# A decoder layer on one core: rotary on 128 partitions with rows moved by DMA, decays by one addition, squares on ScalarE, longer waits in the delta rule

## The chip, the cores and the metric

The kernel runs on one core of a Trainium2 chip. The metric is the device time of one execution in microseconds. Five engines work side by side, each on its own queue in order: TensorE (PE, with its weight loads PEld), VectorE (DVE), ScalarE (ACT), GpSimd (POOL) and SyncE (SP). SP, ACT and POOL also issue DMA transfers; here SP loads the weights and POOL moves small tiles about.

## The reference, cut to what matters

One layer of a hybrid decoder, 256 tokens of width 2048, all in float32:

```python
h = rms_norm(x, ln1)
proj = h @ w_in                     # GDN q|k|v, beta, decay, gate z, MoBA q|k|v, two branch gates
y_a = gated_deltanet(...) @ w_branch_a       # 8 heads of 128, chunks of 64
y_b = moba_attention(partial_rope(q), partial_rope(k), v) @ w_branch_b
x = x + (sigmoid(gate_a) * y_a + sigmoid(gate_b) * y_b) @ w_out
x = x + gated_mlp(rms_norm(x, ln2))          # width 5632, causal conv of 3
out = rms_norm(x, final_norm)
```

Two pieces of it are touched by the change. Partial rotary turns the first 32 of each head's 128 dimensions, with x1 the first 16 and x2 the next 16, and an angle of position times frequency:

```python
rot = concatenate([x1 * cos - x2 * sin, x2 * cos + x1 * sin])
```

The delta rule works on differences of summed decays: `gamma = exp(where(causal, gc[c] - gc[s], -inf))`, then a triangular solve per chunk, a running state, and a normalisation of each head's output by the mean of its squares.

## The kernel before, in words

Activations lie with channels on the 128 partitions and the 256 tokens along the free dimension. Every float32 product is made of three faster ones: a weight block of 128x2048 comes in by SP (L123), ACT rounds it to a high part wh (L113), DVE subtracts to get the low part wl (L110, two instructions of 128x1024 per block), and PE adds high x high, high x low and low x high (L103, 48 matmuls per output block of 128 channels). High and low parts have two buffers each, the raw weight four.

The layer runs in this order: the first projections and the norm; four groups of two delta-rule heads (q, k, v and z, `gdn` and `z` in the names); four groups of two MoBA heads (`moba` for q and k, `v` for v); 16 blocks of gates; the two branch products (`br`); the output product (`wo`); the MLP (`up`, `pd`). Beside this stream of large matmuls stand generators: `decay` (L371), one `gdn` per group (L439), `rotary` (L320) and one `moba` per group (L658). A generator writes a few instructions and yields. The function `tick` (L95) advances every living generator by one step, and it is called each time the main stream has written matmuls worth 1700 units, that is every 16 matmuls of 256 columns. `yield from wait(n)` lets n such steps pass.

The order so written isn't the order on the engines. `TileContext(nc, schedule_with_timeline_sim=True)` has a planner that walks through the program with its own idea of each instruction's time, and gives each engine the instruction written earliest among those it believes ready. On the chip that order is fixed, and an instruction that turns out not to be ready holds up all that stands behind it on its engine. A tile with a `tag` shares its buffers with the other tiles of that tag; a new one waits until an old one is released.

What the change and the prediction's steps touch:

- `rotary` loads the positions into `posi` (48 partitions x 256, in the buffer of tag `ot`, L321-322), makes angles on partitions 0 to 15 and 32 to 47, reduces them by multiples of 2 pi in some thirty DVE steps (`turns`, `less`), and takes sine and cosine on ACT (L365-368).
- `moba` turns q and k (L659-663): two DVE products of 16x512 into `rt`, a POOL product of 48x512 with the cosine and a POOL addition. The columns of the q and k weights are permuted on the host so that x1 and x2 stand at partitions 0 and 32. Three waits later come the scores (L669).
- `gdn` brings two rows of the summed decays to all partitions (`gam`, L441), squares q on POOL (`sqq`, L443), sums the squares on PE (`ssq`), makes three blocks of decay differences per head with six DVE instructions (L454-458, with the columns `cols` and the causal mask `nm`) and one exponential (L459).
- The triangular solve goes through DRAM several times: `X` to `dX` to `Xr` (L528, L530), then `rows` (L534-536) uses `Xr` at L547, four waits after L546; `dE`, `E` and `UB` follow (L550-556), and the chain of products L584 to L604 (`w0`, `z0`, `w1`).
- At the end of a group `ot` is squared on POOL and summed on DVE (L614-615), scaled (L616-619), and after four waits (L620) transposed on PE (`pot`, L624).

Of the kernel before, what the change touches and what calls it, by code (L numbers as in the profile page):

```python
# [11 lines left out]
F32 = mybir.dt.float32  # L12
F32R = mybir.dt.float32r
I32 = mybir.dt.int32
# [5 lines left out]
P = 128  # L20
# [19 lines left out]
def const_array():  # L40
# [3 lines left out]
    c["nm"] = np.where(i[None, :] >= i[:, None], 0.0, -30000.0)  # L44
# [9 lines left out]
    invf = np.zeros((P, 1))  # L54
    invf[:16, 0] = inv
    invf[32:48, 0] = -inv
    c["invf"] = invf
# [18 lines left out]
def layer_kernel(ctx: ExitStack, tc: tile.TileContext, xT, pos, cst, vec, convw, ffw, bdv,  # L76
# [226 lines left out]
    sint = fk.tile([48, T], F32, name="sint")  # L303
    cost = fk.tile([48, T], F32, name="cost")
    rem = cost[:16, :P]
# [5 lines left out]
    rt = fk.tile([48, 2, T], F32, name="rt")  # L311
    pool.memset(rt, 0.0)
# [7 lines left out]
    def rotary():  # L320
        posi = g.tile([48, T], I32, name="posi", tag="ot", bufs=1)  # L321
        sp.dma_start(posi, pos)
        ang = m.tile([48, T], F32, name="ang", tag="s_")
        dve.tensor_copy(ang, posi)
        dve.tensor_scalar(ang, ang, C["invf"][:48, :], None, op0=ALU.mult)
        qn = m.tile([48, T], F32, name="qn", tag="s_")
# [9 lines left out]
        lo1 = m.tile([48, T], F32, name="lo1", tag="pT_")  # L336
        lo2 = m.tile([48, T], F32, name="lo2", tag="pT_")
# [27 lines left out]
        act.activation(sint, ang, AF.Sin)  # L365
        act.activation(cost, ang, AF.Sin, scale=0.5)
        dve.tensor_tensor(cost, cost, cost, op=ALU.mult)
        dve.tensor_scalar(cost, cost, -2.0, 1.0, op0=ALU.mult, op1=ALU.add)


    def decay():  # L371
# [27 lines left out]
        pool.dma_start(dG, gc)  # L399
        dve.tensor_scalar(rem, gc[:, :P], gc[:, P - 1:P], -1.0, op0=ALU.subtract, op1=ALU.mult)  # L400
# [8 lines left out]
        dve.tensor_copy(cols.rearrange("p a b -> p (a b)"), pt[:, :112])  # L409

# [14 lines left out]
    dG = dr.tile([16, T], F32, name="dG", bufs=1)  # L425
    S1 = fk.tile([P, 2, P], F32, name="S1")
# [5 lines left out]
    def dram(t, offset, *ap):  # L432
        return bass.AP(tensor=t.tensor, offset=t.offset + offset, ap=[list(x) for x in ap])

    def wait(n):
        for _ in range(n):
            yield

    def gdn(h0, kq, v):  # L439
# [3 lines left out]
        pool.tensor_tensor(sq, kq[:, 1], kq[:, 1], op=ALU.mult)  # L443
# [7 lines left out]

        for j in range(2):
            c = 8 + h0 + j
            dve.scalar_tensor_tensor(gam[:, j, 2, :], gam[:, j, 1, :], cols[:, 1, c:c + 1], nm,  # L454
                                     op0=ALU.subtract, op1=ALU.min)
            dve.tensor_scalar(gam[:, j, 1, :], gam[:, j, 1, :], cols[:, 2, c:c + 1], 0.0, op0=ALU.add, op1=ALU.min)
            dve.scalar_tensor_tensor(gam[:, j, 0, :], gam[:, j, 0, :], cols[:, 0, c:c + 1], nm,
                                     op0=ALU.subtract, op1=ALU.min)
        act.activation(gam, gam, AF.Exp)  # L459
# [86 lines left out]
        yield from wait(4)  # L546
# [67 lines left out]
        pool.tensor_tensor(so, ot, ot, op=ALU.mult)  # L614
        dve.tensor_reduce(st[:, 4, :], so, axis=AX.X, op=ALU.add)
# [4 lines left out]
        yield from wait(4)  # L620
# [37 lines left out]
    def moba(h0, q, k, v):  # L658
        for t in (q, k):  # L659
            dve.tensor_tensor(rt[:16], t[32:48], sint[32:48, None, :].to_broadcast([16, 2, T]), op=ALU.mult)  # L660
            dve.tensor_tensor(rt[32:48], t[:16], sint[:16, None, :].to_broadcast([16, 2, T]), op=ALU.mult)
            pool.tensor_tensor(t[:48], t[:48], cost[:, None, :].to_broadcast([48, 2, T]), op=ALU.mult)
            pool.tensor_tensor(t[:48], t[:48], rt, op=ALU.add)
# [219 lines left out]
def blocks(w, cw=P):  # L883
    k, n = w.shape
    return w.reshape(k // P, P, n // cw, cw).transpose(2, 1, 0, 3).reshape(n // cw, P, k // P * cw)
# [59 lines left out]
```

## Time and profile before

| | |
|---|---|
| median of 3 runs | 1471.27 us (1469.22 to 1472.8) |
| the profiled execution, its own time | 1470.49 us |
| its span, first to last instruction | 1468.7 us, mean granted TensorE clock 0.996 |
| busy PE, PEld | 1445.5 us (98%), 1387.4 us (94%) |
| busy DVE, ACT, POOL | 971.6 us (66%), 727.1 us (50%), 171.9 us (12%) |
| DMA | 280.52 MB, mean 191 GB/s |

The busy shares are means over stages that differ: the delta rule and MoBA lie between about 40 and 410 us, and the rest is the stream of large matmuls alone. Matmuls are pipelined, so a busy PE is PE with a matmul in flight. The number in brackets behind a row of a timeline is the engine's idle time just before it and what ended it. A plain float32 matmul shows as two instructions.

### The profile page before, as it was taken

To read this page: it belongs to the slowest core of one execution; us is meant where nothing else is said; L and a number is where in the kernel's file an instruction comes from. 1 tells how busy PE (TensorE), PEld (TensorE's weight loads), DVE (VectorE), ACT (ScalarE), POOL (GpSimd) and SP (SyncE) were. 2 spreads that over 40 slices of the span, in tenths; PEclk is the share of its full clock that TensorE was granted. 3 is DMA by queue.
4 is the path that set the end of the run, shared out by engine and by line. 5 is a ranking of instruction groups with operands and counts; after the bars stand their busy time and mean duration, and the time that the engine had idled before them with its cause. 6 is when DMAs were issued, how large, how long until landed. Compare 5 with 4: busy or idle time off the path is not lost.

```text
span 1468.7 us, 26659 instructions
## 1 busy us (share of the span) xinstructions
PE 1445.5 (98%) x11264; PEld 1387.4 (94%) x11264; DVE 971.6 (66%) x1395; ACT 727.1 (50%) x994; POOL 171.9 (12%) x208
## 2 busy tenths in 40 slices
PE   9999999999999999999999999999999999999997
PEld 8999999888999999999999999999999998888886
DVE  7989889886754555766666666666666665554554
ACT  5665673445554444445455544454455454444444
POOL 0023134341230000100100000000000000000000
PEclk9999999999999999999999999999999999999999
DMA  9466554554455555567555555555555555555552
GB/s 338 161 196 200 194 180 154 172 170 156 156 189 191 187 197 201 180 221 262 201 181 193 201 196 186 193 201 193 187 196 201 193 186 173 195 201 195 184 194 86
DMA packets 45319, 280.52 MB, mean 191 GB/s; under 512 B 6544, under 2 KB 7824, under 8 KB 13072
## 3 DMA queue, kind: packets, MB, share of 16 engines
q1 hardware_dynamic: 40272, 270.40, 53.4%
q0 software_dynamic: 4064, 6.26, 1.6%
q10 hardware_dynamic: 864, 2.16, 0.4%
q8 instruction: 88, 1.44, 0.4%
q14 instruction: 31, 0.25, 0.1%
HBM read 275.30 MB, written 3.75 MB: 190 GB/s over the span
## 4 chain that ended last, share of the span: by engine, by line
PE 86%; DVE 6%; DMA 3%; ACT 2%; issue 2%; POOL 1%; SPq 0%; DVEq 0%; POOLq 0%; ACTq 0%
PE ps_up L103 33%; PE pd L91 16%; PE ps_gate L103 12%; PE ps_wo L103 6%; PE ps_br L103 6%; PE ps_gdn L103 4%; PE ps_moba L103 3%; PE ps_v L103 2%; DVE wl L110 2%; PE ps_z L103 2%; DMA wraw<-in_w_gdn 1%; DMA Xr<-dX 1%; ACT wh L113 1%; DMA dX<-X 1%; DVE tm L521 1%
## 5 line engine op out<-in xcount | busy, mean ns | idle before, releaser
L110 DVE TENSOR_TENSOR wl<-wraw,wh 128x1024 fp32r<-128x1024 f32 (+1 forms) x500 | 607.0, 1250 | 183.1 <-ACT wh L113 182.5
L113 ACT CAST wh<-wraw 128x1024 fp32r<-128x1024 f32 (+1 forms) x500 | 496.0, 1040 | 411.2 <-PE ps_up L103 161.0
L103 PE MATMUL ps_up<-h,wh 128*128 128x256 f32 x2816 | 479.4, 276 | 0.0
L103 PEld LDWEIGHTS ps_up<-h,wh 128*128 128x128 f32 x2816 | 424.0, 188 | 0.1
L103 PE MATMUL ps_up<-h,wl 128*128 128x256 f32 x1408 | 388.7, 276 | 0.0
L103 PEld LDWEIGHTS ps_up<-h,wl 128*128 128x128 f32 x1408 | 264.3, 188 | 0.0
L103 PE MATMUL ps_gate<-hc,wh 128*128 128x256 f32 x1024 | 175.5, 277 | 0.0
L103 PEld LDWEIGHTS ps_gate<-hc,wh 128*128 128x128 f32 x1024 | 154.5, 188 | 0.0
L103 PE MATMUL ps_gate<-hc,wl 128*128 128x256 f32 x512 | 141.6, 277 | 0.0
L91 PE MATMUL pd<-wl,ah 128*128 128x512 f32 x336 | 130.8, 389 | 0.0
L91 PE MATMUL pd<-wh,al 128*128 128x512 f32 x336 | 130.8, 389 | 0.0
L103 PE MATMUL ps_gdn<-hc,wh 128*128 128x256 f32 x704 | 125.0, 280 | 0.0
L103 PEld LDWEIGHTS ps_gdn<-hc,wh 128*128 128x128 f32 x704 | 107.6, 189 | 0.4 <-ACT wh L113 0.4
L103 PE MATMUL ps_gdn<-hc,wl 128*128 128x256 f32 x352 | 98.4, 280 | 1.8 <-DVE wl L110 1.8
L103 PEld LDWEIGHTS ps_gate<-hc,wl 128*128 128x128 f32 x512 | 96.1, 188 | 0.1
L103 PE MATMUL ps_moba<-hc,wh 128*128 128x256 f32 x512 | 93.3, 284 | 0.0
L91 PE MATMUL pd<-wh,ah 128*128 128x512 f32 x336 | 92.8, 391 | 0.0
L203 DVE TENSOR_TENSOR unf<-ps_up,R 128x512 f32<-128x512 f32 x44 | 30.4, 692 | 89.0 <-PE ps_up L103 89.0
L103 PE MATMUL ps_wo<-mc,wh 128*128 128x256 f32 x512 | 87.1, 276 | 0.0
L816 POOL TENSOR_TENSOR acts<-sg,cvf 128x256 f32<-128x256 f32 x44 | 32.4, 737 | 459.4 <-ACT sg L815 459.4
L103 PEld LDWEIGHTS ps_moba<-hc,wh 128*128 128x128 f32 x512 | 79.6, 191 | 0.2
L103 PEld LDWEIGHTS ps_wo<-mc,wh 128*128 128x128 f32 x512 | 77.0, 188 | 0.0
(437 smaller groups left out, 1995.7 us busy)
## 6 DMA issues: line engine op xcount, KB each, us to landing
wraw<-in_w_up SPq DMA_DIRECT2D x88, 1024.0 KB, 4.9
wraw<-in_w_dn SPq DMA_DIRECT2D x44, 1024.0 KB, 4.8
wraw<-in_w_gate SPq DMA_DIRECT2D x32, 1024.0 KB, 4.8
wraw<-in_w_gdn SPq DMA_DIRECT2D x30, 1024.0 KB, 5.2
wraw<-in_w_moba SPq DMA_DIRECT2D x16, 1024.0 KB, 4.9
wraw<-in_w_o SPq DMA_DIRECT2D x16, 1024.0 KB, 4.9
wraw<-in_w_mv SPq DMA_DIRECT2D x8, 1024.0 KB, 5.1
wraw<-in_w_ba SPq DMA_DIRECT2D x8, 1024.0 KB, 4.9
```

Source lines behind the costliest of these rows:

```text
L91: pe.matmul(ps, a, b, start=(start and i == 0), stop=(stop and i == n - 1), **kw)
L103: pe.matmul(ps, a, b, start=start, stop=stop, skip_group_check=True)
L110: return (eng or dve).tensor_tensor(lo, src, hi.bitcast(F32), op=ALU.subtract)
L113: act.copy(hi, src)
L203: dve.tensor_tensor(dst, ps, r, op=ALU.mult)
L521: dve.tensor_tensor(tm[:, :, :, :i + 1], Xd[:, :, :, :i + 1], Ad[:, :, None, :i + 1, i].to_broadcast([P, 2, 2, i + 1]), op=ALU.mult)
L816: pool.tensor_tensor(acts[:, c, :], sg, t[:, 1, :], op=ALU.mult)
```

## The change

- The angles are made on 128 partitions x 32 (each frequency on 8 partitions, 32 tokens on each). Sine and cosine go by six transfers of POOL's queue to DRAM and back into `CS`, 64 rows of 128 tokens for q and the same for k.
- `moba` gathers the rows to be turned, x1 and x2 of q and k, by four transfers into `X_`, turns them in five DVE instructions after three waits, and puts them back by four transfers; three waits more, then the scores. The host's permutation goes.
- The decay differences: one addition of the mask for both blocks, and six exponentials with a column as their bias. `cols` holds its first two columns negated for that, by one more DVE instruction in `decay`.
- Both squares of `gdn` go to ACT, the second with the sum in the same instruction, so the reduction on DVE goes.
- The wait ahead of the second `rows` grows from 4 to 6, that ahead of the transposes from 4 to 7.

```diff
-    c["nm"] = np.where(i[None, :] >= i[:, None], 0.0, -30000.0)
+    c["nm"] = np.where(i[None, :] >= i[:, None], 0.0, -1e30)
...
+    c["invf"] = np.repeat(inv, 8)
...
-    sint = fk.tile([48, T], F32, name="sint")
-    cost = fk.tile([48, T], F32, name="cost")
-    rem = cost[:16, :P]
+    CS = fk.tile([P, 2, P], F32, name="CS")
...
-    rt = fk.tile([48, 2, T], F32, name="rt")
-    pool.memset(rt, 0.0)
...
     def rotary():
-        posi = g.tile([48, T], I32, name="posi", tag="ot", bufs=1)
+        posi = m.tile([P, 32], I32, name="posi", tag="pT_")
         sp.dma_start(posi, pos)
-        ang = m.tile([48, T], F32, name="ang", tag="s_")
+        ang = m.tile([P, 32], F32, name="ang", tag="s_")
...
-        act.activation(sint, ang, AF.Sin)
-        act.activation(cost, ang, AF.Sin, scale=0.5)
-        dve.tensor_tensor(cost, cost, cost, op=ALU.mult)
-        dve.tensor_scalar(cost, cost, -2.0, 1.0, op0=ALU.mult, op1=ALU.add)
+        cs = m.tile([P, 2, 32], F32, name="cs_", tag="s_")
+        act.activation(cs[:, 1], ang, AF.Sin)
+        act.activation(cs[:, 0], ang, AF.Sin, scale=0.5)
+        dve.tensor_tensor(cs[:, 0], cs[:, 0], cs[:, 0], op=ALU.mult)
+        dve.tensor_scalar(cs[:, 0], cs[:, 0], -2.0, 1.0, op0=ALU.mult, op1=ALU.add)
+        for a in range(2):
+            for j in range(2):
+                pool.dma_start(dram(dS, a * 32 * T + j * T, (2 * T, 16), (1, T)), cs[:, a])
+        for a in range(2):
+            pool.dma_start(CS[:, a], dram(dS, a * 32 * T, (0, 2), (P, 64), (1, P)))
...
+        rem = m.tile([16, P], F32, name="rem", tag="qk0")
...
         dve.tensor_copy(cols.rearrange("p a b -> p (a b)"), pt[:, :112])
+        dve.tensor_scalar(cols[:, 0:2, :].rearrange("p a b -> p (a b)"), pt[:, :32], -1.0, None, op0=ALU.mult)
...
-        pool.tensor_tensor(sq, kq[:, 1], kq[:, 1], op=ALU.mult)
+        act.activation(sq, kq[:, 1], AF.Square)
...
+        dve.tensor_tensor(gam[:, :, 0::2, :], gam[:, :, 0:2, :], nm[:, None, None, :].to_broadcast([P, 2, 2, P]), op=ALU.add)
         for j in range(2):
             c = 8 + h0 + j
-            dve.scalar_tensor_tensor(gam[:, j, 2, :], gam[:, j, 1, :], cols[:, 1, c:c + 1], nm,
-                                     op0=ALU.subtract, op1=ALU.min)
-            dve.tensor_scalar(gam[:, j, 1, :], gam[:, j, 1, :], cols[:, 2, c:c + 1], 0.0, op0=ALU.add, op1=ALU.min)
-            dve.scalar_tensor_tensor(gam[:, j, 0, :], gam[:, j, 0, :], cols[:, 0, c:c + 1], nm,
-                                     op0=ALU.subtract, op1=ALU.min)
-        act.activation(gam, gam, AF.Exp)
+            for q, a in enumerate((0, 2, 1)):
+                act.activation(gam[:, j, q, :], gam[:, j, q, :], AF.Exp, bias=cols[:, a, c:c + 1])
...
-        yield from wait(4)
+        yield from wait(6)
         rows(Xm, W, Xr, False)
...
-        pool.tensor_tensor(so, ot, ot, op=ALU.mult)
-        dve.tensor_reduce(st[:, 4, :], so, axis=AX.X, op=ALU.add)
+        for p in range(4):
+            act.activation(so[:, p], ot[:, p], AF.Square, accum_out=st[:, 4, p:p + 1])
...
-        yield from wait(4)
+        yield from wait(7)
         pot = r3(sdt("pot"), T)
...
     def moba(h0, q, k, v):
-        for t in (q, k):
-            dve.tensor_tensor(rt[:16], t[32:48], sint[32:48, None, :].to_broadcast([16, 2, T]), op=ALU.mult)
-            dve.tensor_tensor(rt[32:48], t[:16], sint[:16, None, :].to_broadcast([16, 2, T]), op=ALU.mult)
-            pool.tensor_tensor(t[:48], t[:48], cost[:, None, :].to_broadcast([48, 2, T]), op=ALU.mult)
-            pool.tensor_tensor(t[:48], t[:48], rt, op=ALU.add)
+        X_ = m.tile([P, 2, P], F32, name="X_", bufs=1)
+        Xc = m.tile([P, 2, P], F32, name="Xc", bufs=1)
+        Xs = m.tile([P, 2, P], F32, name="Xs", bufs=1)
+
+        def each(f):
+            for a, t in enumerate((q, k)):
+                for b in range(2):
+                    f(t[16 * b:16 * b + 16].rearrange("p j t -> p (j t)"), b, slice(64 * a, 64 * a + 64))
+
+        each(lambda t, b, o: pool.dma_start(X_[o, b], t))
+        yield from wait(3)
+        dve.tensor_tensor(Xc, X_, CS[:, 0:1, :].to_broadcast([P, 2, P]), op=ALU.mult)
+        for b in range(2):
+            dve.tensor_tensor(Xs[:, b], X_[:, 1 - b], CS[:, 1], op=ALU.mult)
+        dve.tensor_tensor(Xc[:, 0], Xc[:, 0], Xs[:, 0], op=ALU.subtract)
+        dve.tensor_tensor(Xc[:, 1], Xc[:, 1], Xs[:, 1], op=ALU.add)
+        each(lambda t, b, o: pool.dma_start(t, Xc[o, b]))
         yield from wait(3)
...
-    perm = np.r_[0:16, 32:48, 16:32, 48:P]
-    perm = (np.arange(H)[:, None] * P + perm).reshape(-1)
...
-        "pos": np.broadcast_to(np.asarray(positions), (48, T)),
+        "pos": np.tile(np.asarray(positions).reshape(8, 32), (16, 1)),
```

More of the change, by code (lines that the diff above doesn't have):

```diff
@@ L53, in const_array @@
     inv = np.float32(500000.0) ** (-np.arange(16, dtype=np.float32) / np.float32(16))
[L54 to L57, printed above, removed]
+    c["invf"] = np.repeat(inv, 8)
     return np.concatenate([c[n].reshape(P, -1) for n, _ in CONST_FIELDS], axis=1).astype(np.float32)
@@ L320, in rotary @@
     def rotary():
-        posi = g.tile([48, T], I32, name="posi", tag="ot", bufs=1)
+        posi = m.tile([P, 32], I32, name="posi", tag="pT_")
         sp.dma_start(posi, pos)
-        ang = m.tile([48, T], F32, name="ang", tag="s_")
+        ang = m.tile([P, 32], F32, name="ang", tag="s_")
         dve.tensor_copy(ang, posi)
-        dve.tensor_scalar(ang, ang, C["invf"][:48, :], None, op0=ALU.mult)
-        qn = m.tile([48, T], F32, name="qn", tag="s_")
+        dve.tensor_scalar(ang, ang, C["invf"], None, op0=ALU.mult)
+        qn = m.tile([P, 32], F32, name="qn", tag="s_")
         MAGIC = 1.5 * 2 ** 23
@@ L334, in less @@
             dve.scalar_tensor_tensor(dst, qn, -part, dst, op0=ALU.mult, op1=ALU.add)
-        lo1 = m.tile([48, T], F32, name="lo1", tag="pT_")
-        lo2 = m.tile([48, T], F32, name="lo2", tag="pT_")
+        lo1 = m.tile([P, 32], F32, name="lo1", tag="pT_")
+        lo2 = m.tile([P, 32], F32, name="lo2", tag="pT_")
         yield
@@ L425, in layer_kernel @@
     dG = dr.tile([16, T], F32, name="dG", bufs=1)
+    dS = dr.tile([2, 32, T], F32, name="dS", bufs=1)
     S1 = fk.tile([P, 2, P], F32, name="S1")
@@ L909 @@
     o += W
-    mq, mk = (blocks(w_in[:, o + i * W:o + (i + 1) * W][:, perm]) for i in range(2))
+    mq, mk = (blocks(w_in[:, o + i * W:o + (i + 1) * W]) for i in range(2))
     mv = w_in[:, o + 2 * W:o + 3 * W]
```

## The prediction

> **What bounds the kernel now.** I read the busy time by stage first, then TensorE's waits, then what each waited for. The view of stages (columns: start and end in us, length, then busy us and instructions of PE, PEld, DVE, ACT and POOL, granted clock, DMA share, GB/s):
>
> ```profile
> 40.00:120.00 80.00, 78.92 (x682) 78.01 (x682) 72.14 (x153) 51.68 (x64) 11.16 (x17) 1.00 0.53 177
> 120.00:210.00 90.00, 86.26 (x715) 84.61 (x714) 76.77 (x166) 55.59 (x87) 31.66 (x53) 0.98 0.57 186
> 210.00:260.00 50.00, 49.18 (x364) 46.52 (x363) 46.43 (x110) 25.68 (x38) 17.65 (x27) 1.00 0.53 179
> 260.00:340.00 80.00, 73.27 (x530) 68.95 (x529) 67.33 (x114) 35.60 (x61) 33.43 (x30) 0.98 0.47 159
> 340.00:410.00 70.00, 69.89 (x534) 66.76 (x533) 45.17 (x79) 38.64 (x70) 10.21 (x6) 1.00 0.48 165
> 410.00:1460.00 1050.00, 1050.00 (x8205) 1007.96 (x8204) 633.66 (x731) 495.02 (x637) 64.44 (x65) 1.00 0.56 192
> ```
>
> From 410 us on PE never stops, and the change touches nothing there. So all it can win lies between 40 and 410 us. There PE idles 1.08 + 3.74 + 0.82 + 6.73 + 0.11 = 12.5 us, while DVE is busy 72.14 + 76.77 + 46.43 + 67.33 + 45.17 = 308 of 370 us. TensorE's waits in that stretch (total us, times, longest):
>
> ```profile
> PE pot L624 <- DVE ot L619: 3.8, 2, 2.0
> PE w L584 <- DVE vb L604: 2.9, 1, 2.9
> PE ps_z L103 <- DVE wl L110: 1.1, 1, 1.1
> PE ps_gdn L103 <- DVE wl L110: 1.1, 2, 0.8
> PE ps_moba L103 <- DVE wl L110: 0.9, 1, 0.9
> PE ps_v L103 <- DVE wl L110: 0.8, 1, 0.8
> PE pT L688 <- DVE s__3503 L682: 0.7, 1, 0.7
> PE py L563 <- issue: 0.6, 1, 0.6
> PE w L594 <- DVE vb L591: 0.6, 1, 0.6
> ...
> 185.00:190.00 5.00, 5.00 (x27) 4.59 (x26) 4.93 (x17) 0.73 (x1) 3.76 (x7) 0.66 0.65 217
> 284.00:289.00 5.00, 5.00 (x32) 5.00 (x31) 4.69 (x14) 2.58 (x5) 0.17 (x1) 0.66 0.56 205
> ```
>
> Nearly every wait is for DVE. The last two rows show a second price: after the two longest stalls (2.0 us for L619, 2.9 us for L604) the granted clock is 0.66 over 5 us, which loses 0.34 x 5 = 1.7 us each. The other stalls cost no clock. The ceiling is 12.5 + 3.4 = 15.9 us. The 1.1 us at ps_z falls in the start of the decay arithmetic, which stays, so 14.8 us are in reach.
>
> **Rotary angles (L320-368).** Two things are late now. The positions are loaded into a buffer shared with ot (L321), which the previous group still holds, and moba's first rotation then waits for the sine and for POOL:
>
> ```profile
> 269.54 0.68 DVE L660 TENSOR_TENSOR rt<-qk,sint 16x512 f32<-16x512 f32 x1 [2.15 <-ACT sint L365]
> 277.14 0.68 DVE L660 TENSOR_TENSOR rt<-qk,sint 16x512 f32<-16x512 f32 x1 [2.36 <-POOL qk L663]
> ...
> L334 DVE SCALAR_TENSOR_TENSOR ang<-qn,ang 48x256 f32<-48x256 f32 x10 | 4.1, 408 | 0.1
> L521 DVE TENSOR_TENSOR tm<-X,Xa 128x32 f32<-128x32 f32 x4 | 0.8, 212 | 0.0
> ```
>
> The 33 DVE steps go from 48x256 to 128x32, so from about 0.408 to 0.212 us: 33 x 0.196 = 6.5 us. The tile posi moves to a buffer that the decays leave early, so the chain can fill DVE's gaps long before 269.54 us, where its sine is waited for now. The six transfers of the table (16 KB and more, on POOL's queue, six issues) must only be in before the first moba rows; cs and CS have tens of us. If that cover were gone, the first rotation would wait for two landings, some 9 us by the longer landing below. With it the 2.15 and 2.36 us of DVE idling go, and with them the L604 stall: 2.9 + 1.7 = 4.6 us, and perhaps the 0.8 us at ps_v. **Taken: 5.0 us of gain**, bounds 0 to 5.4.
>
> **Rotation of q and k (L658-663).** Removed per group: four DVE operations of 0.68 us and four POOL operations. Added: eight small transfers on POOL's queue and five DVE operations, one of 128x256 and four of 128x128.
>
> ```profile
> 369.52 0.68 DVE L660 TENSOR_TENSOR rt<-qk,sint 16x512 f32<-16x512 f32 x1
> 370.92 3.43 DVE L110 TENSOR_TENSOR wl<-wraw,wh 128x1024 fp32r<-128x1024 f32 x2
> 381.27 2.36 DVE L110 TENSOR_TENSOR wl<-wraw,wh 128x1024 fp32r<-128x1024 f32 x2 [0.19 <-ACT wh L113]
> L565 DVE TENSOR_TENSOR Y<-py,ct 128x256 f32<-128x256 f32 x4 | 1.6, 411 | 0.0
> L591 DVE TENSOR_TENSOR vb<-vb,z 128x128 f32<-128x128 f32 x8 | 2.2, 280 | 3.7 <-PE z L590 3.6
> L555 POOL DMA_DIRECT2D UB<-dE x32 | 17.1, 543 | 1.9 <-DVE s__3473 L682 1.1 <-DMA E<-dE 0.9
> UB<-dE POOLq DMA_DIRECT2D x32, 8.0 KB, 3.3
> S<-dA POOLq DMA_DIRECT2D x16, 8.0 KB, 4.7
> 383.79 0.69 DVE L203 TENSOR_TENSOR qk<-ps_moba,R 128x512 f32<-128x512 f32 x1 [0.15 <-PE ps_moba L103]
> L669 PE MATMUL sc<-qk,qk x4: 377/377/378, 392.2 to 394.9; 128*128 128x256 f32 x4
> L669 PE MATMUL sc<-qk,qk x16: 377/379/382, 312.6 to 394.9; 128*128 128x256 f32 x16
> ```
>
> DVE: 4 x 0.68 - (0.411 + 4 x 0.280) = 1.2 us saved per group, 4.8 us in all. The wl pair at 370.92 took 3.43 us while POOL rotated, against 2.36 without: 1.07 us for each of eight rotations, 8.6 us of DVE. POOL gives up its arithmetic for 8 x 0.543 = 4.3 us of issuing per group. The stalls behind this slow DVE, in the stage from 260 us, are 0.6 + 0.9 + 1.7 (the second L619) + 0.7 = 3.9 us. **Taken: 2.7 us of gain** (seven tenths, since other late work stands there too), bounds 0 to 3.9.
>
> The Trainium skill (SBUF — State Buffer, "Who interferes with whom") speaks against these transfers: POOL's descriptor writing is locked out while DVE runs an operation that takes both ports. The L555 row does not bear it out, with 0.543 us over 32 issues in stages where DVE was 84 to 93% busy.
>
> The new price is the way there and back. After the last join (k): two issues 1.1, landing 3.3 to 4.7, DVE 1.5, four issues 2.2, landing 3.3 to 4.7, together 11.4 to 14.2 us before the score matmul can start. In group 3 it starts now at 392.2, 8.4 us after the join at 383.79, so it comes 3 to 6 us later. PE has gate matmuls to go on with, and loses only what the written order did not foresee: bounds 0 and 5.8 + 1.7 = 7.5 us. **Taken: 1.0 us of loss**, near the lower end, since the planner puts a matmul behind the landing it reckons with. Group 0's first score stands at 312.6, 35 us after its second rotation began (277.14); groups 1 and 2 follow it with the same arrears, and that cover hides the trip. Without it each costs what group 3's does. DVE, too, waits for the landed rows four times; each is like L534 below, 2.5 us, 10 us of DVE at most against some 25 us freed. **Taken: 1.0 us of loss**, bounds 0 and 4 x 0.9, the price of a late wl.
>
> The Trainium skill (DMA: Bandwidth & Descriptors, "Anatomy of one DMA") gives a small transfer about 2.0 us. By that the trip is 8.8 us and the 1.0 us at the scores falls away; the measured 3.3 and 4.7 us decide against it.
>
> **Longer waits (L546, L620).** Each wait is 16 matmuls, 1.9 us by the first stage's row (80 us / 682).
>
> ```profile
> DVE tw L534 <- DMA Xr<-dX: 7.6, 3, 4.2
> 181.41 1.02 DVE L534 TENSOR_TENSOR tw<-W,Xr 128x512 f32<-128x512 f32 x1 [4.20 <-DMA Xr<-dX]
> 182.34 0.69 DVE L619 TENSOR_TENSOR ot<-ot,st 128x512 f32<-128x512 f32 x1
> ```
>
> L619, for which PE stalled 2.0 us, stood behind L534, which waited 4.20 us for Xr. Two waits more (3.8 us) would cover two of the three L534 waits whole and most of the third; three more at L620 put the transposes behind it. But the rotation of group 3's q ran at 369.52, though its generator starts only behind the join of k at 383.79: the planner follows readiness, and the written place is only a priority. What such an edit moves is uncertain: between nothing and 2.0 + 1.7 + 0.8 (wl after it) + 0.6 (py) + 0.2 = 5.4 us. **Taken: 2.2 us of gain**, two fifths. Behind the moved operations only their own group's chain comes later; the next user of those buffers is a group away.
>
> **Decays and squares (L442-459, L613-615).**
>
> ```profile
> L454 DVE SCALAR_TENSOR_TENSOR gam<-gam,cols,ct 128x128 f32<-128x128 f32 x8 | 2.8, 346 | 1.0 <-DMA gam<-dG 1.0
> L615 DVE TENSOR_REDUCE st<-so 128x4 f32<-128x512 f32 x4 | 2.7, 684 | 2.2 <-POOL so L614 2.2
> L586 ACT COPY w<-w 128x128 f32<-128x128 f32 x8 | 2.1, 267 | 8.7 <-PE w L584 8.6
> L421 ACT ACTIVATE kq<-kq 128x512 f32<-128x512 f32 x8 | 5.1, 633 | 6.5 <-DVE st L450 4.4 <-DVE kq L418 2.0
> L459 ACT ACTIVATE gam<-gam 128x768 f32<-128x768 f32 x4 | 3.4, 847 | 0.0
> ```
>
> DVE drops four operations like L454 and two smaller ones for one addition of 0.69 us (L619's shape), and the 0.684 us reduction: per group 1.38 - 0.69 + 0.68 = 1.4 us or more. With the terms above DVE is freed of 6.5 + 4.8 + 8.6 + 5.5 = 25 of 308 us, the relief behind the gains already taken. ACT gains six exponentials for one (6 x 0.267 - 0.847 = 0.75), a square of 0.633 and four of at least 0.267: 2.5 us per group, 6.1 if each small one cost 0.633. That is 10 to 24 us on an engine busy 207 of 370 us, in its idle time. If it delays wh, wl is late by some 0.9 us per group. **Taken: 0.5 us of loss**, bounds 0 and 3.6. The extra operation on the new cols columns is one 0.15 us step.
>
> **Sum.** -5.0 - 2.7 - 2.2 + 1.0 + 1.0 + 0.5 = -7.4 us. The profiled execution took 1470.49 us; the median, 1471.27, is 0.8 higher. From the profile 1463.1, from the median 1463.9: I forecast **1464**.
>
> **Rivals.**
> - *The stalls move.* DVE still runs 283 of 370 us and the order is planned anew, so stalls come back elsewhere: half of the gains (5.0) less losses of 4 give 1470. For it: the eleven stalls have many causes. Against: the two that cost clock have causes the change removes.
> - *The landings stop PE (slower).* Freed of the late sine, all four groups reach their scores as soon as the planner believes the rows landed, and PE stands at L669 for L534's mean lateness, 2.5 us, plus 1.7 us of clock: 4 x 4.2 = 16.8 against 9.9 of gains, 1478. It is slower from 3.2 us per group, clock included. Against: today's tens of us of cover in three groups.
> - *POOL's issues are starved.* If each waits out one wl of 1.2 us, the six behind k's join take 7 us more; group 3 stalls some 6 us, 1470. [...]
> - *All goes well.* All 14.8 us return: 1456.5. For it: the shared cause, DVE. Against: the Xr landings stay.
>
> **Chances.** Forecast 0.57 (own range 1458 to 1468), moving stalls 0.17, landings 0.13, starved issues 0.03, all well 0.10. About 0.2%, 2.9 us, is what a measurement can tell from no change. Faster is the forecast, the good case and a little of the first rival, 0.67; same 0.17; slower, the landings and the tail of the first, 0.16. The range, 1457 to 1474, leaves out the landings' case and half of the best.
>
> **What would show it.** Right: no POOL arithmetic between 270 and 390 us, single wl near 1.2 us there, no wait on sint, no 0.66 clock near 284 us, PE's waits in 40 to 410 us near 5 us. Wrong: PE waiting at the score matmul for a DMA, DVE waiting on X_ for more than 10 us, new table loads between the exponentials, or wl waiting for ACT far beyond today.

## The result

| | median us | executions | profiled: time, span |
|---|---|---|---|
| before | 1470.24 | 1469.22, 1472.8, 1471.27, 1467.78 | 1470.49, 1468.7 |
| after | 1454.40 | 1454.32, 1454.49, 1454.32, 1458.98 | 1454.32, 1452.5 |

The medians differ by 15.8 us; the ratio is 0.9900 (95% interval 0.9873 to 0.9926), which is 14.7 us of 1472, between 10.9 and 18.7. In a second series the same kernel took 1454.9 to 1458.4 us, median 1456.88, ratio 0.9888 (0.9871 to 0.9904). The forecast was 1464 with a range from 1457 on. The sign is right; the gain is twice the forecast, and the medians of both series lie under the range, the second by 0.1 us.

**Profile after.** The view by stage, same columns as in the prediction:

```profile
40.00:120.00 80.00, 78.52 (x674) 77.31 (x673) 72.88 (x174) 55.35 (x78) 12.73 (x21) 1.00 0.55 181
120.00:210.00 90.00, 90.00 (x769) 89.51 (x769) 79.41 (x168) 64.53 (x112) 29.58 (x51) 1.00 0.60 197
210.00:260.00 50.00, 50.00 (x349) 46.35 (x348) 39.82 (x86) 24.12 (x40) 19.36 (x35) 1.00 0.62 204
260.00:340.00 80.00, 80.00 (x583) 75.36 (x582) 52.33 (x107) 38.59 (x77) 16.80 (x31) 1.00 0.55 182
340.00:410.00 70.00, 70.00 (x594) 69.30 (x593) 43.49 (x77) 46.60 (x82) 14.66 (x15) 1.00 0.43 144
```

TensorE's idle time between 40 and 410 us fell from 12.5 to 1.48 us, all of it ahead of 120 us, and the granted clock is 1.00 throughout. TensorE's and DVE's waits in that stretch (L107, L110 and L533 of this kernel are L110, L113 and L534 of the kernel before):

```profile
PE ps_z L100 <- DVE wl L107: 1.5, 2, 1.3
...
DVE wl L107 <- ACT wh L110: 28.5, 23, 7.7
DVE Xs L671 <- DMA X__3396<-qk: 2.6, 1, 2.6
DVE tw L533 <- DMA Xr<-dX: 0.9, 1, 0.9
```

One stall of TensorE worth the name is left (1.3 us), the one at ps_z that the prediction took to stay. DVE's first row reads, in the kernel before:

```profile
DVE wl L110 <- ACT wh L113: 13.9, 9, 3.3
```

DVE waits for the landing Xr for 0.9 us in place of 7.6, and for landed rows X_ once. Some operations by groups, and transfers with the time to their landing in the last column:

```profile
L327 DVE SCALAR_TENSOR_TENSOR ang<-qn,ang 128x32 f32<-128x32 f32 x10 | 1.8, 184 | 0.0
L458 ACT ACTIVATE gam<-gam,cols 128x128 f32<-128x128 f32 x24 | 7.5, 390 | 0.6 <-DVE gam L454 0.6
L667 POOL DMA_DIRECT2D X__4212<-qk x4 | 2.0, 513 | 16.8 <-DVE qk L200 12.9 <-DVE mx L691 3.9
...
wraw<-in_w_gdn SPq DMA_DIRECT2D x30, 1024.0 KB, 5.0
X__4212<-qk POOLq DMA_DIRECT2D x4, 32.0 KB, 1.8
qk<-Xc POOLq DMA_DIRECT2D x16, 32.0 KB, 3.6
```

A step of the angles takes 0.184 us (0.212 was reckoned), a small exponential 0.390 (0.267).

**Where the time came from.** The rows of idle time leave out that a matmul after a stall also starts its successor late. I therefore took the starts of all matmuls from the trace and counted, for each gap to the next start, what it has beyond the median gap of that shape of matmul. Half clock is in it too. Sums in us, each from the one profiled execution of its kernel:

```
                     60-180 180-240 240-290 290-340 340-410   sum
before                 3.7     6.4     6.3     6.4     3.8    26.6
after                  3.3     1.2     0.9     1.9     3.3    10.6
after, 2nd series      6.2     1.3     0.8     1.6     3.7    13.5
early only             5.2     6.1     2.6     8.9     4.8    27.5
short only             3.1     3.9     2.3    10.9     3.3    23.6
short and early        3.1     3.0     0.9     5.1     3.7    15.8
new rotary (with turn) 7.8     1.2     0.9     1.8     3.8    15.5
squares only           2.7     2.3     1.6     9.5     4.1    20.3
before, new order      3.7    11.4     3.4     7.6     3.8    29.8
after, new order       9.4     4.6     0.8     2.1     3.2    20.1
```

The 16.0 us between before and after are the 16.2 us of span. Nearly all of them come out of three stretches: 5.2 us from 180 to 240, 5.4 from 240 to 290, 4.5 from 290 to 340. The lower rows belong to the experiments. The table ends at 410 us. In "early only", "short and early", "new rotary" and "squares only" some 1.5 to 3 us more than before are lost behind it, about 2 of them where the gate matmuls from 415 to 460 us start every 0.118 us in place of 0.113; the reason for that is open.

### The profile page after: what moved, and what is told of

It is laid out like the page before. It is cut to its first block, busy times and chain, and to the rows that moved or that the text cites. A ratio compares the mean times of both kernels' runs of the same rounds, so it can differ in the third digit from the quotient of the medians.

```text
span 1452.5 us, 26727 instructions
## 1 busy us (share of the span) xinstructions
PE 1440.8 (99%) x11264; PEld 1385.4 (95%) x11264; DVE 942.5 (65%) x1376; ACT 738.8 (51%) x1050; POOL 150.1 (10%) x221
## 4 chain that ended last, share of the span: by engine, by line
PE 95%; ACT 2%; DMA 1%; DVE 1%; issue 0%; SPq 0%; DVEq 0%; ACTq 0%
PE ps_up L100 33%; PE pd L88 17%; PE ps_gate L100 12%; PE ps_gdn L100 7%; PE ps_moba L100 6%; PE ps_wo L100 6%; PE ps_br L100 6%; PE ps_v L100 3%; PE ps_z L100 2%; DMA wraw<-in_w_gdn 1%; PE g L88 1%; DVE wl L107 0%; ACT wh L110 0%; PE ps_bd L88 0%; PE po L88 0%
## 5 line engine op out<-in xcount | busy, mean ns | idle before, releaser
L107 DVE TENSOR_TENSOR wl<-wraw,wh 128x1024 fp32r<-128x1024 f32 (+1 forms) x500 | 599.1, 1236 | 193.7 <-ACT wh L110 193.3
L110 ACT CAST wh<-wraw 128x1024 fp32r<-128x1024 f32 (+1 forms) x500 | 496.1, 1040 | 417.4 <-PE ps_up L100 160.6
L110 ACT CAST ah<-acts 128x256 fp32r<-128x256 f32 x44 | 17.9, 407 | 119.2 <-PE pd L88 118.3
```

What stands on the lines that cost most here:

```text
L107: return (eng or dve).tensor_tensor(lo, src, hi.bitcast(F32), op=ALU.subtract)
L110: act.copy(hi, src)
```

## The experiments

All ratios are to the kernel before, run on the same chip.

| kernel | median us | ratio (95%) |
|---|---|---|
| before with the longer waits | 1471.32 | 0.9993 (0.9982-1.0004) |
| before with the decays | 1472.16 | 0.9993 (0.9980-1.0005) |
| before, angles short, late | 1471.34 | 0.9990 (0.9976-1.0004) |
| before, angles long, early | 1475.63 | 1.0021 (1.0008-1.0035) |
| before, new order only | 1474.51 | 1.0012 (1.0003-1.0021) |
| before with the squares | 1467.05 | 0.9956 (0.9939-0.9973) |
| before with the new rotary | 1461.56 | 0.9922 (0.9904-0.9940) |
| before, angles short and early | 1459.85 | 0.9916 (0.9896-0.9935) |
| after, second series | 1456.88 | 0.9888 (0.9871-0.9904) |
| after, old waits | 1456.84 | 0.9888 (0.9864-0.9912) |
| after, old turn, new angles | 1457.15 | 0.9902 (0.9887-0.9917) |
| after, POOL's work put back | 1460.19 | 0.9902 (0.9872-0.9933) |
| after, old squares | 1458.53 | 0.9918 (0.9900-0.9935) |
| after, rows sent a longer way | 1461.87 | 0.9922 (0.9897-0.9948) |
| after, old rotary | 1461.80 | 0.9929 (0.9902-0.9956) |
| after, new order only | 1462.14 | 0.9933 (0.9912-0.9955) |
| after, 22 us more on DVE | 1463.88 | 0.9935 (0.9910-0.9959) |
| after, decay's ACT work later | 1466.35 | 0.9965 (0.9951-0.9979) |

### The two halves and the waits

Theory A: the parts add up as in the prediction. Theory B: the stalls have one common cause, a late DVE, so that several parts each take most of them. Four kernels: the waits alone undone; the whole rotary undone (angles, turn, layout of the weights, load); the rotary alone done; the waits alone done.

```
after_waits4 / before_waits: L546 wait(6) <-> wait(4), L620 wait(7) <-> wait(4)
after_rot_old: after without, before_rot: before with, the parts of the diff
  in const_array, rotary(), moba(), dS, "pos" and the permutation
```

> The whole change with the two waits back at 4. Theory A (each part removes its own stalls, as the prediction summed them): 2.2 us of the gain are lost, about 1456.6 us, and a stall at the transposes L624 comes back. Theory B (the planner follows readiness, the written place hardly counts): within 1 us of 1454.4, and no PE wait above 0.3 us between 60 and 410 us.

> The whole change without its rotary part: angles and rotation of q and k as before, with the new decays, squares and waits. Theory A: 1471.3 - 2.2 + 0.5 = 1469.6 us. Theory B (the stalls have one common cause, DVE being late, and the rotary part brings four fifths of DVE's relief): the stalls from 250 us on return with their loss of clock, the ones before 210 us do not, 1462 to 1467 us.

> The kernel before with only the new angles and the rows moved by DMA. Theory A: 1471.3 - 5.0 - 2.7 + 2.0 = 1465.6 us. Theory B: nearly all stalls from 210 us on go (9.4 us with their clock), those at 134 to 198 us stay or change: 1457 to 1461 us.

> The kernel before with only the two longer waits. Theory A: 1471.3 - 2.2 = 1469.1 us, and up to 5.4 us of gain if L619 really moves ahead of L534. Theory B: the stall of 2.0 us at L624 and its half clock stay where they are, within 1 us of the kernel before.

Measured: 1456.84, 1461.80, 1461.56 and 1471.32 us. The waits are worth nothing that can be measured, done (from 2.6 us of gain to 0.6 of loss) or undone. The traces show why: with and without them DVE's instructions stand in the same order up to 324 us in the kernel before, and up to 342 us in the kernel after. The stall at L624 that B expected to stay was all the same absent from the profile with the waits alone; the last section says why. The rotary alone is worth 11.5 us (0.78% of 1472), all other parts together 10.5, and both together about 15: they do not add, as B said. Of these two runs B's ranges missed the times by 0.2 and 0.6 us, A's figures by 7.8 and 4.0. B itself had to be tested further.

### The angles: early, short, or both

Three kernels take the rotary's 11.5 us apart; the old turn on DVE and POOL stays in all three.

```
before_early:    -posi = g.tile([48, T], ..., tag="ot")   +posi = m.tile([48, T], ..., tag="pT_")
before_ang:      -posi = g.tile([48, T], ..., tag="ot")   +posi = m.tile([P, 32], ..., tag="pT_")
                 ang, qn, lo1, lo2 as [P, 32]; sine, -sine, cosine to dS, from there to sint and cost (7 DMAs)
before_ang_late: as before_ang, but +posi = g.tile([P, 32], ..., tag="ot")
```

> The kernel before with one edit: the positions go into a buffer of the pool m (tag pT_), free early, instead of the one that ot holds, so that the angles can be worked out before the third quarter of the stretch. Everything else of the old rotary stays. Theory A (the sum): the angles' term, less the 6.5 us of DVE that the 128 partitions save: no wait on sint, no stall at L604 with its half clock, 4.6 us less, about 1466.5. Theory B (one common cause, DVE being late from 210 us on): taking the 33 steps out of the crowded stretch from 243 to 268 us lets the work behind them come early and most stalls from 210 us on go, 6 to 9 us less, 1461.5 to 1464.5. If the load time of the positions is nothing: 1471.

> The kernel before with the angles alone changed: worked out on 128 partitions from an early load and handed to the old tables sint and cost by seven small transfers. The rotation itself stays the old one, two DVE and two POOL operations for q and for k. Angles early on 48 partitions alone gave 1475.6 against 1473.7, so the early start by itself gains nothing. Theory A (the sum): 6.5 us less of DVE and no wait on sint, 5.0 us less, about 1468. Theory B1 (the whole of the rotary's 11 us hangs on the DVE time of the angles): 1461 to 1464. Theory B2 (the stalls move wherever DVE work is moved, as after the early start alone, and the 11 us come from the new rotation): 1471 to 1475.

> The angles alone on 128 partitions, as in the run that gave 1459.85, but with the positions loaded into the buffer that ot holds, so that the chain starts late, after 240 us, as in the kernel before. Early start alone was worth +1.9 us, short and early -12.6. If the shorter DVE time counts wherever it stands: 1460 to 1464. If short steps need the early start: the first rotation waits for the sine and now for the table's two landings too, 1469 to 1474. By the prediction's price for a lost cover, some 9 us at the first rotation, it would be 1469 as well.

Measured: early 1475.63, short and early 1459.85, short 1471.34. So the angles alone hold most of the whole change's gain, 12.4 us (9.6 to 15.3), and more than twice the term's upper bound of 5.4, but only if they are short and early. Early alone lost 3.1 us (1.2 to 5.2), short alone can't be told from nothing (3.5 us of gain to 0.6 of loss). The table by stretches says where. From 240 to 290 us, where the sine was awaited, each removes most of the loss (6.3 to 2.6, 2.3 and 0.9), as the prediction had it. Early or short alone gives back a good part or all of that from 290 to 340 us (8.9 and 10.9 in place of 6.4). TensorE and DVE with the early, long angles, then with the short, late ones:

```profile
327.13 0.69 DVE L615 TENSOR_REDUCE st<-so 128x4 f32<-128x512 f32 x1 [2.82 <-POOL so L614]
328.50 0.69 DVE L619 TENSOR_TENSOR ot<-ot,st 128x512 f32<-128x512 f32 x1
...
329.33 1.09 PE L624 MATMUL pot<-ct,ot 128*128 128x128 f32 x4 [4.54 <-DVE ot L619]
```
```profile
314.45 0.25 DVE L564 STREAM_TRANSPOSE Et<-E 128x64 f32<-128x64 f32 x1 [3.73 <-DMA E<-dE]
...
314.80 1.04 PE L568 MATMUL py<-Et,S 128*128 128x32 f32 x4 [3.38 <-issue]
```

In both, DVE stands at an instruction whose partner is late (POOL's square, the landing E), with what TensorE needs queued behind it. These stalls are not leftovers of the angles; by the traces, other instructions of the same kernel met late partners in the new order.

### Decays and squares, each alone

```
before_decay: the diff's lines for nm, cols and L454-459    before_sq: those for L443 and L614-615
```

> The kernel before with the decays alone changed: one DVE addition of the mask and six exponentials with a bias on ACT, in place of six DVE operations and one exponential. Theory A: a small loss from ACT, 0.3 us at most, 1471 to 1471.5. Theory B: DVE is the late engine in every delta-rule group, 1.4 us less of it per group takes 1 to 4 us from the stalls at L619 and py: 1467 to 1470. A rival, ACT delays wh: 0.9 us per group, 1474.9.

> The kernel before with the squares alone moved: sqq on ACT in place of POOL, the squares of ot on ACT with their sums in place of POOL and one DVE reduction. Theory A: within 0.5 us of before. Theory B: DVE no longer waits for POOL at L615 (2.2 us over four groups) and is freed of the 0.684 us reduction and of the stretching beside POOL, so that the stalls at L619 (3.8 us with the half clock 5.5) shrink: 1466 to 1469. A rival, the ACT work delays wl: slower by up to 3.6 us, 1474.9.

Measured: decays 1472.16, nothing that can be told; squares 1467.05, 6.5 us less (4.0 to 9.0), inside B's range, where A had nothing. In the profile with the squares on ACT one large stall is left:

```profile
297.33 1.02 DVE L534 TENSOR_TENSOR tw<-W,Xr 128x512 f32<-128x512 f32 x1 [5.29 <-DMA Xr<-dX]
...
299.10 1.09 PE L624 MATMUL pot<-ct,ot 128*128 128x128 f32 x4 [5.33 <-DVE ot L619]
```

Undone in the kernel after:

> The kernel after with the squares on POOL and the reduction on DVE again, all else new. Alone, the squares were worth 6.7 us. Theory A (the sum): a gain of 0.5 us by undoing them, 1454. Theory B (one common cause, DVE late; the rest of the change has already relieved it): within 1.5 us of after. Theory D (each stall has its own place; DVE at L615 waits for POOL's square with ot and wl behind it, whatever the angles do): 2 to 6 us lost, 1456.5 to 1460.5.

Measured: 1458.53 (1455.05 to 1461.34). That is 1.7 us above the second series of the kernel after by the medians, 4.4 by the ratios, and within what a mere new order did (next section), so what the squares are worth once the angles are short stays open.

### What a new order does by itself

An edit can make the planner lay out all that follows anew. Two kernels change only that, with a wait of nine ahead of the products with Xr; here the order does change, from 141 us on in the kernel before and from 160 us on in the kernel after:

```
-        yield from wait(4)      (after: wait(6))
+        yield from wait(9)
         rows(Xm, W, Xr, False)
```

> The kernel before with a wait of nine in place of four ahead of the products with Xr: no arithmetic changes, and the order of DVE's instructions is new from the first group's solve (about 137 us) on. If before owes its time to the work that it does (the long angles, the squares by way of POOL): 1468 to 1476, with stalls at other places. If it was an unlucky order: 1460 to 1467.

> The kernel after with a wait of nine in place of six ahead of the products with Xr. No arithmetic changes; the order of DVE's instructions is the same up to the first group's solve and other from there on, since the planner lays out the later groups anew. It measures what a new order alone does. If the gain of the change is a matter of work taken away, any such order gives 1453 to 1459. If it is a matter of the order that the planner happened on: stalls come back at new places, 1460 or more. The late landing at 135 us, which costs 4.6 us in some executions, lies ahead of the first difference and stays.

> The kernel after, unchanged, in five rounds on one chip with before. If the late landing at 135 us strikes in one execution of four: a lowest time of 1454.3 and a median within 0.3 us of it, with a few at 1458 to 1460. If it strikes as often as in the runs with the waits or POOL's work put back (two and three of four): a median between 1456 and 1459.

Measured: 1474.51 for before, 1462.14 for after, against 1456.88 for the unchanged kernel after in its second series. Before's time doesn't look like an unlucky order: it and five kernels close to it (the waits, the decays, early, short, the new order) take 1470 to 1476. The kernel after seems a fortunate order of its work: the one new order tried costs 6.6 us by the ratios against the second series (the intervals 0.9912 to 0.9955 and 0.9871 to 0.9904 do not meet) and 4.9 against the first, whose interval it overlaps. Not all of that is the order's. The profile, of the slowest of the four executions (1464.65), shows a late landing at 133 us, ahead of the first change of order, and two new stalls behind it:

```profile
133.10 1.07 DVE L533 TENSOR_TENSOR tw<-W,Xr 128x512 f32<-128x512 f32 x1 [5.26 <-DMA Xr<-dX]
...
202.10 0.38 PE L100 MATMUL ps_gdn<-hc,wl 128*128 128x256 f32 x1 [1.69 <-DVE wl L107]
214.93 0.49 PE L589 MATMUL z<-w,S 128*128 128x128 f32 x2 [0.89 <-ACT w L585]
```

What the order itself did is nearer to 3.5 us: in the table the stretch with the two stalls, 180 to 240 us, has 3.4 us more than in the kernel after, and the fastest execution (1458.12) lies 3.8 us above after's fastest. The rest fits the landing, which strikes the unchanged kernel too. Order and landing together moved a median by up to 6.6 us, so no single change of the kernel after that moves it by less than some 7 us can be put down to the work it edits. This bounds all that follows.

### The turn, POOL's work, DVE's load, the way of the rows

```
after_turn_old:  X_, Xc, Xs and their transfers out; the old four operations on sint, cost for q and k in
after_pool_back: +for t in (q, k): twice pool.tensor_tensor(t[64:112], t[64:112], ones, op=mult)
after_dve_load:  in wait(10), per slot: +2 x dve.tensor_tensor(jk, aq0[:, 0, 0, :P], ident, op=mult)
after_trip:      -pool.dma_start(t, Xc[o, b])   +Xc -> dX1 -> dX2 (DRAM), then from dX2[o, b]
```

> The kernel after with the turn of q and k alone undone: the angles stay on 128 partitions and early, their table is handed to sint and cost as in the run of the angles alone, and q and k are turned by two DVE and two POOL operations each; decays, squares and waits are the new ones. Theory A (the sum): the rotation's term comes back, 2.7 less the two losses of 1.0, so 1455 to 1457. Theory D (the stalls are places where DVE stands at a late partner, and only the angles and the squares took such places away): the new turn has no part, 1453 to 1456. If the turn by transfers is what removes the last stalls: 1459 or more.

> The kernel after with POOL arithmetic put back beside the new rotary: per group, q and k are each multiplied twice by ones on POOL, 48 partitions by 512, over partitions that the rotation does not touch; the values stay. It gives back the POOL work that the old rotary did, without any other part of it. If DVE is stretched beside POOL as the pair wl was before (3.43 against 2.36 us), 8.6 us of DVE return over the four groups. Theory A: PE loses what the prediction took for this, about 2.7 us, with the score matmuls 3 to 4 us later in each group: 1457 to 1458. Theory B: DVE has enough slack left after the change, or its lateness is covered: within 1 us, 1454 to 1455.5. If the contention was the main cost of the old rotary: 5 us or more, 1459.5 and above.

> The kernel after with 20 products of 128x128 put on DVE in each group of the delta rule, spread over the ten slots of one wait; nobody reads them. At about 0.28 us each they are 5.6 us per group, 22 us in all, as much as the change freed by the prediction's count (25 us). Theory B (DVE's freed time is the common cause): the stalls come back, two thirds of the gain or more is lost, 1464 to 1470. A rival, what counts is which instructions wait for POOL, ACT and landings, not DVE's load: DVE has slack after the change and PE loses 2 us at most, 1454 to 1457. In some executions of the kernel after (one of four) a late landing at 135 us costs 4.6 us; such a step is not counted as the load's.

> The kernel after with the rotated rows sent over two more places in DRAM before they come back into q and k: two more transfers in a row per group, so the rows land later by two landings and two issues, 5 to 10 us by the 1.8 to 3.6 us that X_ and qk took to land. Theory A (the landings lie open at the scores, as the loss term and its rival have it): PE stands at the score matmuls in the four groups, 3 us or more each, 1464 or above. Theory B (work of other groups covers the trip): within 1.5 us of after, 1454 to 1456.

Measured: 1457.15, 1460.19, 1463.88, 1461.87 us.
- The turn by transfers has no part that can be told from nothing: undone, 2.1 us more by the ratios, and the intervals overlap.
- POOL's work put back: one execution took 1454.38, as fast as the kernel after; the profiled one lost most of its time between 136 and 142 us, ahead of any rotation. Between 180 and 400 us four of its wl instructions beside POOL took 2.07 to 2.44 us in place of 1.15, and TensorE waited for none of them. In the kernel before there were seven such, so the run gives back about half of that stretching.
- 22 us more on DVE cost 7 us, as much as the new order with its landings (0.9935 and 0.9933). The time lies just under theory B's range. That DVE's load as such is the common cause isn't shown, and isn't ruled out.
- The longer way: no wait of TensorE at the score matmuls in its profile. That is of the fastest execution (1456.87); where the other three, at 1461.7 to 1463.8, lost their time is not known. What the profiled one lost stood at a landing of the delta rule again:

```profile
278.50 1.02 DVE L534 TENSOR_TENSOR tw<-W,Xr 128x512 f32<-128x512 f32 x1 [5.31 <-DMA Xr<-dX]
279.43 1.20 DVE L604 TENSOR_TENSOR vb<-vb,r 64x128 f32<-64x128 f32 x4
...
280.45 0.46 PE L584 MATMUL w<-vb,UB 128*128 128x128 f32 x2 [2.52 <-DVE vb L604]
```

### A try at the stall that is left

```
-            if gr == 0 and a == 1: bg.append(decay())      (now behind z's chunk)
+        with tc.issue_after(casts[11].ins): act.activation(beta, z0, AF.Sigmoid)   (and the exponential)
```

> The kernel after with the decay written behind z's chunk and its two table functions on ACT (sigmoid, exponential) held behind the casts of z's second block. It aims at the one stall of TensorE that the profile after still shows, ps_z waiting 1.3 us for wl at 54 us, which the product of the casts' ACT time with three table loads makes. If ACT's delay is the cause: the stall goes, 1.3 to 1.5 us less, 1452.9 to 1453.2. If the decays are wanted early: the gain is lost at the first delta-rule group, 1454 to 1457.

Measured: 1466.35. The profile is of the slowest of ten executions (1473.02), so its sizes are not those of the median. The stall at 54 us went (between 40 and 60 us the loss, counted as above, fell from 1.7 to 0.2 us), so the decays' work there had caused it. But the decays then come late. DVE stands 4.54 us at their landing; the exponentials of both heads follow on ACT with other functions between them, each change with a row ACT_TABLE_LOAD, a table load of 1.28 us; and the weights' casts behind all of it keep TensorE waiting 5.28 us. The table loads that the prediction feared among the exponentials are found here, and not in the kernel after, whose 24 exponentials have four:

```profile
86.85 0.69 DVE L457 TENSOR_TENSOR gam<-gam,ct 128x512 f32<-128x512 f32 x1 [4.54 <-DMA gam<-dG]
...
88.89 1.28 ACT L485 ACT_TABLE_LOAD   x1
...
90.80 1.28 ACT L461 ACT_TABLE_LOAD   x1
...
96.40 0.79 PE L100 MATMUL ps_gdn<-hc,wh 128*128 128x256 f32 x2 [5.28 <-ACT wh L110]
```

No kernel beat the kernel after.

## Why the prediction was wrong

- **"What bounds the kernel now"** held: TensorE waiting for DVE between 40 and 410 us, nothing from 410 on. The ceiling of 14.8 us "in reach" was a little low: from 60 us on TensorE's idle time sums to 11.4, the start-to-start gaps of the eleven stalls there to 13.2, some 0.16 us more for each, and with the two half clocks (3.4) that is 16.6; the table above has 16.0 fewer after the change.
- **Rotary angles, -5.0, bounds 0 to 5.4: the step that failed, mis-sized.** Alone it measured -12.4 (-9.6 to -15.3). At its own place it was right (5.4 us between 240 and 290 us, the bound). The bound left out what the same edit can win or lose elsewhere. In the profile 3.4 us came back from 180 to 240 us, where the prediction had seen a stall at L619 behind the wait for Xr and given it to the waits' term. What was gone there was the wait for a landing that took 2.8 us less (last section). That needs no edit: with the longer waits alone, and DVE's order unchanged up to 324 us, the same landing was short and the same stall absent. So part of the -12.4 may be where landings happened to fall; how much stays open. That an early start alone, which the text priced as the main part, gains nothing was not foreseen either.
- **Longer waits, -2.2: not borne out.** Nothing that can be told from zero, and DVE's order hardly changed. The working had the reason in it (the planner follows readiness) and took two fifths all the same. Of a wait that the planner does not heed, nothing should have been taken. (A wait of nine it did heed.) The term's upper bound adds up to 5.3, not 5.4, which changes nothing.
- **Decays and squares, +0.5: the sign was wrong for the squares.** The quoted row of L615 showed DVE standing 2.2 us at POOL's square, and the sum counted only the reduction's 0.684 us. Alone the squares are worth 6.5 us. ACT's extra work (DVE's wl waited for it 28.5 us in place of 13.9) did not reach TensorE, except perhaps for 0.2 us more at ps_z. The decays' part, near nothing, held.
- **Rotation of q and k, -2.7, and its two losses of 1.0:** POOL's rows between 270 and 390 us are gone, as foreseen, but neither gain nor loss could be measured. TensorE waited for no landing at the scores in the profiles, even with two more transfers in a row; the wait on X_ was 2.6 us once and stopped nothing.
- **The rivals.** "All goes well", 1456.5 with a chance of 0.10, is where the result lies (1454.4 and 1456.9). The reason held against it, that the Xr landings stay, holds for some executions and not for others. "POOL's issues are starved" did not come: an issue of X_ takes 0.51 to 0.53 us. The Trainium skill (SBUF — State Buffer, "Who interferes with whom"), which the prediction set against these transfers, does not say that of wl: by it `tensor_tensor`, which wl is, has no two-port mode, and was not seen to stall a DMA. These rows agree. The landings' rival and "the stalls move" did not come for the whole change; the second came for several parts alone.
- **The sum.** The forecast took fractions of each group of stalls, as if each part could win only the stalls nearest to it. The parts measured alone give -12.4, -6.5 and about nothing for the rest, 19 us where 15 to 16 were to be had: the two large ones must share stalls. How the surplus over the forecast divides between angles and squares inside the whole change is not shown. (In the chances, 0.67 for faster is the forecast's 0.57 and the good case's 0.10; nothing is left in it for the first rival.)

**What stays open.** How much of after's 15 us is its fortunate order. By the new orders of both kernels the work itself is worth 1474.5 - 1462.1 = 12 us, but that is one order each, with the landings' scatter in it.

## What to carry to other kernels

Where one engine's queue feeds TensorE, ask at each instruction that waits for a partner (a landing, another engine's square) what stands behind it in that queue: the stalls that the traces here show stand at such places. Whether the engine's load counts beside them is not settled. Before giving a few us to an edit in a planned kernel, time an edit that only makes the planner order anew; here that, with the scatter of landings, was worth up to 6.6 us. And cost an edit for the whole stretch that it lies in: the angles lost 3.1 us made early, won nothing that can be told made short, and won 12.4 made both.

## What was not expected of the hardware

The same small load, Xr (its landing is counted from the start of its issue on POOL), lands after 2.3 or after 5 us, and by the traces which of the two hangs on where it falls against the weights' 1 MB transfers on SP's queue. Before, then with the short and early angles, at the same place of the program:

```profile
176.00 0.33 SPq L123 DMA_DIRECT2D wraw<-in_w_gdn  x1
176.22 0.56 POOL L530 DMA_DIRECT2D Xr<-dX  x1 [2.48 <-DMA dX<-X]
```
```profile
176.76 0.57 POOL L535 DMA_DIRECT2D Xr<-dX  x1 [1.87 <-DMA dX<-X]
177.74 0.33 SPq L120 DMA_DIRECT2D wraw<-in_w_gdn  x1
179.15 1.08 DVE L539 TENSOR_TENSOR tw<-W,Xr 128x512 f32<-128x512 f32 x1 [0.52 <-DMA Xr<-dX]
```

Issued 0.22 us behind a weight transfer, Xr landed after 5.2 us, and DVE stood 4.20 us (L534 at 181.41, quoted in the prediction); issued 0.98 us ahead of one, after 2.4 us, and DVE stood 0.52. The kernel after does both, in its first and in its second series:

```profile
125.07 0.52 POOL L529 DMA_DIRECT2D Xr<-dX  x1 [1.65 <-DMA dX<-X]
126.50 0.33 SPq L120 DMA_DIRECT2D wraw<-in_w_gdn  x1
127.41 1.05 DVE L533 TENSOR_TENSOR tw<-W,Xr 128x512 f32<-128x512 f32 x1
```
```profile
127.17 0.53 POOL L529 DMA_DIRECT2D Xr<-dX  x1 [2.86 <-DMA dX<-X]
127.37 0.33 SPq L120 DMA_DIRECT2D wraw<-in_w_gdn  x1
132.23 1.06 DVE L533 TENSOR_TENSOR tw<-W,Xr 128x512 f32<-128x512 f32 x1 [3.89 <-DMA Xr<-dX]
```

The kernel before does the same where nothing was edited ahead of it. With the longer waits, in the same order of DVE's instructions, the load fell ahead of the weight transfer, and TensorE's stall at L624 with its half clock (2.0 and 1.7 us) did not come:

```profile
176.90 0.56 POOL L530 DMA_DIRECT2D Xr<-dX  x1 [1.88 <-DMA dX<-X]
177.28 0.33 SPq L123 DMA_DIRECT2D wraw<-in_w_gdn  x1
179.28 1.08 DVE L534 TENSOR_TENSOR tw<-W,Xr 128x512 f32<-128x512 f32 x1 [0.79 <-DMA Xr<-dX]
```

Over 20 profiles with 80 loads of Xr: 15 were issued between 1.3 us after and 0.25 us before the start of a weight transfer's issue, and landed after 3.7 to 5.8 us, median 5.0, about what the weight transfer itself takes (5.0). The other 65 took 2.2 to 3.8 us (one 6.2), median 2.4. Of the 3.6 us between the two profiled executions of the kernel after, 2.9 lie between 60 and 180 us, where this landing stands. Between the kernel before and the one with the longer waits, 0.6 us of shift against the weight transfer (0.22 behind it, 0.38 ahead) was enough to make or remove the stall.

The trace's records of single DMA pieces show what held the load. A weight transfer is 128 pieces of 8 KB, Xr 32 of 4 KB. Before, the pieces of the transfer issued at 176.00 start between 176.99 and 180.37 us, those of Xr between 180.04 and 180.84. With the short and early angles Xr's start between 178.02 and 178.49, and the weights' only from 178.68 on. In the ten loads issued behind a weight transfer, at most 1.3 us after it, whose pieces can be told apart, 118 or more of the 128 weight pieces had started before the first of Xr. The Trainium skill (DMA: Bandwidth & Descriptors, "Queues, rings and completion order") has each DMA engine take turns between queues packet by packet, with about 9 to 17 descriptors to a packet. If each piece is one descriptor and they are spread evenly, an engine's share of a weight transfer is 128 / 16 = 8, an estimate; that fits into one packet, so the rule has Xr wait for all of it, as seen. No run moved a weight transfer on purpose or changed its pieces, so this is read from the traces, not tested.

A second thing: the length of a stall doesn't tell whether half clock follows it. In the runs here idles of 1.77 us (early only) and 1.81 us (after, old waits) were followed by 3.4 us of half clock, while idles of 2.53 us (rows sent a longer way) and 2.60 us (early only) were not. So the prediction's "two longest stalls" described its profile and is no rule to carry on.
